# The order of the delta rule's pairs of heads: 1, 2, 0, 3 in place of 1, 2, 3, 0

## The chip, the cores and the metric

The kernel runs on one core of a Trainium2 chip. The metric is the time of one execution on the device in microseconds (us), smaller is better. A core has TensorE (PE; its weight loads are listed apart as PEld), VectorE (DVE), ScalarE (ACT), GpSimd (POOL) and SyncE (SP), which here issues nearly all DMAs; 16 DMA engines carry them out. TensorE's clock has two levels, 1.2 and 2.4 GHz; the profile gives the granted share of the full one.

## What is computed

One layer of a decoder for 288 tokens (256 of a prompt, and 8 sequences of 4 tokens with stored state) at width 2048, all in float32. A normed input is multiplied by one wide matrix `w_in`; the columns feed three mixers, whose outputs are gated, merged and followed by a feed-forward part:

```python
h = rmsnorm(x)                        # 288 x 2048
P = h @ w_in                          # 2048 x 16416: columns split among the mixers
# RetNet: rq 512, rk 512, rv 1024, rg 1024        (columns 0 to 3071)
# gated delta rule: q 1024, k 1024, v 1024         (3072 to 6143), da 8, db 8, dz 1024 (6160)
# GLA: lq 512, lk 512, lv 1024, llr 16, lg 1024    (7184 to 10271), then gates 6144
y_ret, y_gdn, y_gla = ...             # each 288 x 1024
merge = sum_i sigmoid(gate_i) * (branch_i @ w_branch[i])
x = x + merge @ w_o
x = x + SwiGLU(rmsnorm(x))
```

The gated delta rule has 8 heads of 128 columns. For each head q, k and v go through a convolution of width 4 over time and a SiLU, q and k are normed, and a state of 128 x 128 per sequence is read, used and written back. The heads don't depend on each other.

## The kernel before

Weights stream from HBM once. A product `x_in` (256 columns of `w_in`) is made by `products`: it loads four pieces `raw` of 512 KB (each 128 partitions x 4 rows x 256 columns, so 1 KB at a time out of rows of 16,416 x 4 = 65,664 bytes), splits each into a high and a low float32r part (`wh` by a ScalarE cast, L422; `wl` by a VectorE subtraction, L135), and multiplies with three matmuls per block (L129), 96 matmuls of 128 x 128 x 288 in all. `halves` does the same for 512 columns, in pieces of 2 KB. Four `raw` buffers are there, so the loads run at most four pieces ahead; SyncE issues them, in the order of its queue, with the state loads and stores and the small transfers between them.

`run` goes through four rounds. Each calls `self.gdn(ORDER[n])` for a pair of heads and then half of RetNet or GLA: (RetNet 1), (RetNet 0), (GLA 1), (GLA 0). `gdn(pair)` makes four products, for q, k, v (`gdn_conv`, columns 3072, 4096 and 5120 plus 256 x pair) and the gate (`gated`, columns 6160 plus 256 x pair), and then starts a generator `gdn_mix` with the delta rule itself. RetNet and GLA make a query and a key product and two of 512 columns, and start generators for their heads too. The generators do their small steps between the dense matmuls: `pump` advances them once per block of the following products. So the delta rule of one pair runs beside the products that follow it, and beside the delta products of the third round run RetNet's last heads, beside those of the fourth GLA's first heads.

`ORDER[0]` stays the same and is used three times more: the first pair's query weights are loaded in `setup`, and `gates` follows its second product. A pair number enters only as a column, row or index: in the weight columns, in the state (`state_gdn[0, :, h]`, 512 KB a head, loaded and stored by SyncE), in the convolution's state rows (ScalarE's queue, 24 KB), and in the block `ys[1, h]` of a scratch tensor in HBM to which `finish` writes a head's output. `branch(1, ...)` reads these blocks in the order of heads 0 to 7, after `branch(0, ...)`; the first two of these reads are issued early, as two `yr` buffers come free. For GLA, `gla` loads sums of the forget gate from HBM (`ev<-fsum`, L1279), and every head's state goes through four buffers `s0`, so that a state load (L659, L1073) waits for an earlier state's store to land.

The order of instructions on each engine is made by a scheduler from dependencies and modelled lengths; the program is one straight line without branches.

Of the kernel before, what the change touches and what calls it, by code (L numbers as in the profile page):

```python
# [39 lines left out]
R1 = 4  # L40
R2 = 6
EV = 9
ORDER = (1, 2, 3, 0)

O_RQ, O_RK, O_RV, O_RG = 0, 512, 1024, 2048
O_GQ, O_GK, O_GV = 3072, 4096, 5120
# [51 lines left out]
def blocks(t):  # L98
    return [t[:, k] for k in range(t.shape[1])]


class Trunk:
# [74 lines left out]
    def setup(self):  # L177
# [24 lines left out]
        for n in range(D // XC):  # L202
# [7 lines left out]
            ks = slice(2 * (n % 2), 2 * (n % 2) + 2)  # L210
            nc.sync.dma_start(out=raw[:, ks], in_=self.w_in(O_GQ + ORDER[0] * CHUNK)[:, 2 * n:2 * n + 2])
        xd = self.t(self.dr, (KT, P, T), "xT")
# [42 lines left out]
        for _ in range(2):  # L255
            next(steps)
        self.early = self.products(blocks(self.xh), blocks(self.xl), self.w_in(O_GQ + ORDER[0] * CHUNK), KT, False, steps, False)
        ra = self.t(x0, (112, P), "ra")
# [699 lines left out]
    def gdn(self, pair):  # L958
        q = self.gdn_conv(pair, 0)
        k = self.gdn_conv(pair, 1)  # L960
        if pair == ORDER[0]:
            self.gates()
# [486 lines left out]
    def run(self):  # L1449
# [7 lines left out]
        for n, (f, pair) in enumerate(((self.ret, 1), (self.ret, 0), (self.gla, 1), (self.gla, 0))):  # L1457
            self.gdn(ORDER[n])
            if n == 0:
# [67 lines left out]
```

## Time and profile before

| | us |
|---|---|
| median of 3 runs | 2231.0 (2226.45 to 2235.02) |
| profiled execution | 2233.02 |
| its span | 2231.2 |
| second round: pair 2 and RetNet 0, from the first matmul of its first product | 204.8 to 385.1 |
| third round: pair 3 and GLA 1 | 385.1 to 569.5 |
| fourth round: pair 0 and GLA 0 | 569.5 to 767.0 |

A round's stages below begin with the first matmul of a product. The rows are from one profiled execution. A window row gives its length, then for each engine its busy time and the number of instructions, then the granted share of TensorE's clock (PEclk), the mean busy share of the 16 DMA engines, and the GB/s that they moved. In a waits row the first engine stood idle until the second was done: us in total, times, longest. In a timeline row the numbers are start and length, and in brackets the idle time before it and what ended it. Matmuls overlap, so one that is listed with 0.29 us starts 0.13 us after the one before.

### The profile page before, as it was taken

The page shows a single profiled execution, that of the slowest core. Times are in us where ns is not written, and L with a number is a line of the kernel's source. Part 1 is how long each engine was busy: PE and PEld are TensorE (multiplying, and loading weights), DVE is VectorE, ACT ScalarE, POOL GpSimd, SP SyncE. Part 2 cuts the span into 40 slices and gives each one's busy share as a digit, 9 for nine tenths or more (in the row PEclk, how much of TensorE's full clock was granted, in tenths as well). Part 3 has the DMA queues.
Part 4 walks back from the last instruction along what each step waited for, and adds up shares of the span by engine and source line. Part 5 has one row for each costly group of instructions (what it writes and reads, how often), then busy time and mean ns, then how long its engine had stood idle before and what let it go on. Part 6 is the DMA issues. An engine that isn't in the chain of part 4 may idle for free.

```text
span 2231.2 us, 43877 instructions
## 1 busy us (share of the span) xinstructions
PE 2173.9 (97%) x17020; PEld 2114.5 (95%) x17020; DVE 1350.2 (61%) x2952; ACT 1028.7 (46%) x2114; POOL 211.7 (9%) x264
## 2 busy tenths in 40 slices
PE   8999989999998999999999999999999999999997
PEld 7899989989888999999999999999999999999997
DVE  6876775685686586555565655565555445556544
ACT  5645543553454355444444444444444334444443
POOL 2102301231343042000000000000000000000000
PEclk9999999999999999999999999999999999999998
DMA  8737985865997666677676566555555555555553
GB/s 232 159 117 160 159 177 115 196 168 127 129 135 181 122 197 185 190 188 186 176 191 164 169 183 187 176 163 169 166 165 168 164 169 162 170 162 169 162 161 118
DMA packets 251512, 370.24 MB, mean 166 GB/s; under 512 B 20318, under 2 KB 120248, under 8 KB 251144
## 3 DMA queue, kind: packets, MB, share of 16 engines
q1 hardware_dynamic: 249200, 364.04, 64.0%
q8 instruction: 133, 2.18, 0.4%
q0 software_dynamic: 896, 2.45, 0.3%
q10 hardware_dynamic: 1208, 0.96, 0.2%
q14 instruction: 75, 0.61, 0.1%
HBM read 341.70 MB, written 25.69 MB: 165 GB/s over the span
## 4 chain that ended last, share of the span: by engine, by line
PE 87%; DMA 8%; DVE 2%; ACT 1%; issue 1%; SPq 1%; POOL 0%; POOLq 0%; DVEq 0%; ACTq 0%
PE pd L129 54%; PE pm L129 32%; DMA raw<-in_w_in_dram 5%; PE pm L126 1%; DMA yr<-ys 1%; DMA out_dram<-s 1%; DVE wl L135 1%; DMA ev<-fsum 1%; ACT wh L422 0%; DMA xb<-in_x_sample_dram 0%; DMA s<-in_state_ret_dram 0%; DVE r L135 0%; DVE r L144 0%; SPq L204 0%; POOL r L1220 0%
## 5 line engine op out<-in xcount | busy, mean ns | idle before, releaser
L135 DVE TENSOR_TENSOR wl<-raw,wh 128x512 fp32r<-128x512 f32 (+1 forms) x1208 | 839.8, 698 | 711.1 <-ACT wh L386 491.0
L129 PE MATMUL pd<-xh,wh 128*128 128x288 f32 x2768 | 825.8, 300 | 22.2 <-ACT wh L422 14.5
L129 PE MATMUL pd<-xl,wh 128*128 128x288 f32 x2768 | 825.5, 299 | 0.0
L129 PE MATMUL pd<-xh,wl 128*128 128x288 f32 x2768 | 817.3, 299 | 1.6 <-DVE wl L135 1.6
L386 ACT CAST wh<-raw 128x512 fp32r<-128x512 f32 x784 | 485.1, 620 | 645.8 <-PE pd L129 332.9
L129 PEld LDWEIGHTS pd<-xh,wh 128*128 128x128 f32 x2768 | 524.5, 190 | 28.1 <-ACT wh L422 15.3
L129 PEld LDWEIGHTS pd<-xl,wh 128*128 128x128 f32 x2768 | 525.5, 190 | 3.5 <-issue 1.2
L129 PEld LDWEIGHTS pd<-xh,wl 128*128 128x128 f32 x2768 | 521.3, 190 | 6.4 <-DVE wl L135 3.5
L355 ACT CAST wh<-raw 128x512 fp32r<-128x512 f32 x224 | 137.8, 618 | 202.3 <-PE pd L129 187.0
L129 PE MATMUL pm<-xh,wl 128*128 128x288 f32 x704 | 207.8, 295 | 0.0
L129 PE MATMUL pm<-xl,wh 128*128 128x288 f32 x704 | 207.3, 294 | 0.0
L129 PE MATMUL pm<-xh,wh 128*128 128x288 f32 x704 | 207.0, 294 | 0.0
L422 ACT CAST wh<-raw 128x512 fp32r<-128x512 f32 x192 | 117.8, 621 | 93.7 <-PE pd L129 53.9
L129 PEld LDWEIGHTS pm<-xh,wl 128*128 128x128 f32 x704 | 132.1, 188 | 0.0
L129 PEld LDWEIGHTS pm<-xh,wh 128*128 128x128 f32 x704 | 132.1, 188 | 0.0
L129 PEld LDWEIGHTS pm<-xl,wh 128*128 128x128 f32 x704 | 132.0, 188 | 0.0
L129 PE MATMUL pd<-ah,wl 128*128 128x288 f32 x352 | 103.9, 295 | 0.0
L129 PE MATMUL pm<-ah,wl 128*128 128x288 f32 x352 | 103.9, 295 | 0.0
L129 PE MATMUL pm<-al,wh 128*128 128x288 f32 x352 | 103.8, 295 | 0.0
L129 PE MATMUL pd<-al,wh 128*128 128x288 f32 x352 | 103.7, 295 | 0.0
L129 PE MATMUL pm<-ah,wh 128*128 128x288 f32 x352 | 103.7, 295 | 0.0
L129 PE MATMUL pd<-ah,wh 128*128 128x288 f32 x352 | 103.6, 294 | 0.0
(372 smaller groups left out, 2921.1 us busy)
## 6 DMA issues: line engine op xcount, KB each, us to landing
raw<-in_w_in_dram SPq DMA_DIRECT2D x252, 512.0 KB
raw<-in_w_gate_up_dram SPq DMA_DIRECT2D x176, 512.0 KB
raw<-in_w_down_dram SPq DMA_DIRECT2D x88, 512.0 KB
raw<-in_w_branch_dram SPq DMA_DIRECT2D x48, 512.0 KB
raw<-in_w_o_dram SPq DMA_DIRECT2D x32, 512.0 KB
out_dram<-s SPq DMA_DIRECT2D x16, 512.0 KB
s<-in_state_gdn_dram SPq DMA_DIRECT2D x8, 512.0 KB
s<-in_state_ret_dram SPq DMA_DIRECT2D x16, 256.0 KB
```

What stands on the lines that cost most here:

```text
L126: self.nc.tensor.transpose(out, in_, self.ident[:k, :k])
L129: self.nc.tensor.matmul(out, lhsT=lhsT, rhs=rhs, start=start, stop=stop)
L135: self.nc.vector.tensor_tensor(out, a, b, op=op)
L355: nc.scalar.copy(wh, src)
L386: nc.scalar.copy(wh, raw[:, k])
L422: nc.scalar.copy(h, src)
```

## The change

The delta rule's pairs run in the order 1, 2, 0, 3. The third round takes pair 0 and the fourth pair 3; the first two rounds, RetNet and GLA stay. The last pair to be written to `ys` is then that of heads 6 and 7.

```diff
@@ -40,7 +40,7 @@
 R1 = 4
 R2 = 6
 EV = 9
-ORDER = (1, 2, 3, 0)
+ORDER = (1, 2, 0, 3)
 
 O_RQ, O_RK, O_RV, O_RG = 0, 512, 1024, 2048
 O_GQ, O_GK, O_GV = 3072, 4096, 5120
```

## Rows read from the trace of the kernel before

**Rows 1.** Page, part 1: busy us (share of the span) xinstructions of each engine.

```profile
PE 2173.9 (97%) x17020; PEld 2114.5 (95%) x17020; DVE 1350.2 (61%) x2952; ACT 1028.7 (46%) x2114; POOL 211.7 (9%) x264
```

**Rows 2.** Page, part 4: the chain that ended last, by line.

```profile
PE pd L129 54%; PE pm L129 32%; DMA raw<-in_w_in_dram 5%; PE pm L126 1%; DMA yr<-ys 1%; DMA out_dram<-s 1%; DVE wl L135 1%; DMA ev<-fsum 1%; ACT wh L422 0%; DMA xb<-in_x_sample_dram 0%; DMA s<-in_state_ret_dram 0%; DVE r L135 0%; DVE r L144 0%; SPq L204 0%; POOL r L1220 0%
```

**Rows 3.** Windows by stage, rounds three and four: us, busy (x) by engine, PEclk, DMA, GB/s.

```profile
385.10:455.40 70.30, 70.30 (x509) 66.53 (x508) 51.32 (x133) 37.09 (x91) 22.57 (x25) 1.00 0.84 191
455.40:499.70 44.30, 38.75 (x271) 34.94 (x270) 36.89 (x124) 25.56 (x77) 16.01 (x19) 0.92 0.64 166
569.50:655.00 85.50, 79.80 (x578) 73.67 (x577) 62.24 (x181) 38.29 (x95) 27.09 (x38) 0.98 1.00 133
655.00:702.50 47.50, 37.99 (x262) 34.51 (x261) 33.01 (x88) 24.39 (x75) 16.57 (x15) 0.93 0.77 177
```

**Rows 4.** Waits in pair 3's stage, 385.1 to 455.4: us in total, times, longest us.

```profile
ACT wh L422 <- DMA raw<-in_w_in_dram: 0.8, 1, 0.8
```

**Rows 5.** Waits in pair 0's stage, 569.5 to 655.0.

```profile
ACT wh L422 <- DMA raw<-in_w_in_dram: 14.6, 8, 5.7
```

**Rows 6.** Windows with 1 KB weight loads: pair 3, pair 0, RetNet's query (column 0).

```profile
371.00:391.00 20.00, 20.00 (x148) 18.12 (x147) 14.09 (x39) 10.08 (x31) 7.44 (x7) 1.00 0.45 92
550.00:570.00 20.00, 20.00 (x150) 17.97 (x150) 12.04 (x33) 9.51 (x28) 6.21 (x7) 1.00 1.00 84
258.00:275.00 17.00, 17.00 (x123) 15.76 (x121) 13.12 (x37) 8.43 (x18) 3.91 (x4) 1.00 0.90 84
```

**Rows 7.** Timeline of SyncE's DMA issues, 531 to 564: start us, us, what, xcount.

```profile
531.20 10.36 SPq L347 DMA_DIRECT2D raw<-in_w_in_dram  x4
547.54 16.02 SPq L325 DMA_DIRECT2D raw<-in_w_in_dram  x4
```

**Rows 8.** Windows with 2 KB weight loads: RetNet's second round, GLA's third.

```profile
303.00:361.00 58.00, 57.56 (x647) 54.82 (x646) 39.92 (x106) 20.17 (x39) 0.57 (x2) 1.00 0.70 142
496.00:545.00 49.00, 49.00 (x604) 46.75 (x603) 30.47 (x82) 18.08 (x36) 5.68 (x8) 1.00 0.47 139
```

**Rows 9.** Windows from a pair's first load to its last: pair 3, pair 0.

```profile
363.00:434.00 71.00, 71.00 (x529) 66.89 (x528) 43.83 (x117) 35.80 (x90) 18.67 (x22) 1.00 0.72 159
547.50:643.90 96.40, 90.81 (x668) 83.36 (x669) 63.47 (x187) 44.51 (x116) 31.46 (x44) 0.98 0.98 123
```

**Rows 10.** Timeline of ScalarE: the cast of pair 0's last load.

```profile
643.98 0.62 ACT L422 CAST wh<-raw 128x512 fp32r<-128x512 f32 x1 [0.20 <-DMA raw<-in_w_in_dram]
```

**Rows 11.** Timeline of TensorE: small matmuls of GLA's heads in pair 0's stage.

```profile
596.57 1.05 PE L129 MATMUL pm<-r 128*128 128x128 f32 x8
600.78 0.33 PE L129 MATMUL pm<-r 128*32 128x32 f32 x8 [2.63 <-DVE st L1249]
```

**Rows 12.** Timeline of the fourth round: the forget sums and who waits.

```profile
671.38 1.11 SPq L1279 DMA_DIRECT2D ev<-fsum  x1
679.35 0.23 ACT L132 ACTIVATE geb<-ev 128x32 f32<-128x32 f32 x1 [12.33 <-DMA ev<-fsum]
680.14 0.61 PE L129 MATMUL pd<-xh,wh 128*128 128x288 f32 x1 [8.03 <-ACT wh L422]
```

**Rows 13.** Window behind that stand: PEclk is the granted clock.

```profile
677.00:683.80 6.80, 3.66 (x14) 3.44 (x15) 3.54 (x9) 4.02 (x11) 0.07 (x1) 0.50 0.49 113
```

**Rows 14.** Timeline of the third round: the same load and its waiters.

```profile
480.68 0.50 SPq L1279 DMA_DIRECT2D ev<-fsum  x1
486.55 0.35 ACT L132 ACTIVATE geb<-ev 128x32 f32<-128x32 f32 x2 [1.35 <-DMA ev<-fsum]
488.75 0.55 PE L126 MATMUL pm<-ident,ev 128*128 128x128 f32 x3 [1.73 <-DVE ev L144]
```

**Rows 15.** Timeline of SyncE: the branches' blocks written (L649) and read (L1297).

```profile
804.80 0.92 SPq L649 DMA_DIRECT2D ys<-yo  x2
822.11 3.83 SPq L1297 DMA_DIRECT2D yr<-ys  x2
```

## The prediction

> **What bounds the kernel now.** I read the page first: TensorE is busy 97% of the span and matmuls are 86% of the chain that ended last, but 5% of that chain is weight loads out of `w_in`, the largest other item [rows 1, 2]. So the mean says "TensorE" and one stage may say something else. The rounds of `run` (one pair of the delta rule, then half of RetNet or GLA) all issue the same dense products, so I cut the span at the first matmul of each product and compared rounds [rows 3]. The reader is to see that the third round's delta stage (pair 3) takes 70.3 us at a DMA share of 0.84, and the fourth round's (pair 0) 85.5 us at a share of 1.00 and *fewer* GB/s (133 against 191). The waits agree: ScalarE's weight casts wait 0.8 us for loads in pair 3's stage and 14.6 us in pair 0's [rows 4, 5].
>
> Why are pair 0's loads slow? Two stretches hold weight loads alone [rows 6]: for pair 3 the DMA engines move 92 GB/s at a share of 0.45, so 92/0.45 = 204 GB/s while they work; for pair 0 it is 84 GB/s at a share of 1.00. Nothing else is issued by SyncE between 531 and 564 us [rows 7], so it isn't company that slows them. What differs is the address: each load takes 1 KB pieces of rows of 16,416 columns, pair p starting at column 256p of its block; pair 0 starts at 3072, 4096, 5120 (multiples of 1024) and 6160 (16 past one), pair 3 768 further. RetNet's query product of the second round starts at column 0, another multiple of 1024, and moves 84 GB/s at 0.90, so 93 [rows 6]. Pieces of 2 KB show it too: starts 1024 and 2048 move 142/0.70 = 203 GB/s, starts 8720 and 9760 (528 and 544 past a multiple) 139/0.47 = 296 [rows 8]. So I take the slowness as the address's, and expect it to go where pair 0 goes.
>
> The Trainium skill, "DMA: Bandwidth & Descriptors", section "Latency and other measured facts", says that copies slow down where partitions lie a large power of two apart in HBM, and that padding by 192 B didn't cure it. This pitch is 64 KiB + 128 B, so by that rule alone all four pairs, which share the pitch, would be equally slow and the order worth 0 (2231). Here the trace disagrees: at one pitch it shows 204 and 84 GB/s, and by these rows I go.
>
> **The change part by part.** No instruction is added or removed; in the third and fourth rounds pair 0 and pair 3 change places. What moves with a pair is its 16 weight loads of 512 KB, two loads and two stores of state, the convolution's small state rows, and the addresses of its outputs.
>
> (a) *Pair 0 in the third round.* From its first load to its last, pair 3's loads and what goes with them take 0.72 x 71.0 = 51.1 us of all 16 engines; pair 0's take 0.98 x 96.4 = 94.5 [rows 9]; the end at 643.9 is the last one's cast, which waited for it [rows 10]. The lead is the same in both rounds: first load to first matmul is 385.1 - 363.0 = 22.1 and 569.5 - 547.5 = 22.0 us [rows 3, 9]. So the supply would again end 96.4 us after 363.0, at 459.4; TensorE needs the 655.0 - 643.9 = 11.1 us after it that it needs now, and the stage ends at 470.5 in place of 455.4: +15.1. The low bound comes from TensorE's work: pair 0's stage holds 578 - 509 = 69 more matmuls than pair 3's [rows 3], since GLA's heads run beside it, and at 0.04 to 0.13 us each (0.33/8 and 1.05/8, [rows 11]) 3 to 9 us of its extra 15.2 are that work, not the loads; the loads alone would then be worth 15.2 - 9 = +6. I take +14, near the supply's figure, because the share stood at 0.98 to 1.00 throughout. Bounds +6 and +16.
>
> (b) *Pair 3 in the fourth round.* Its loads and what goes with them want 51 us of the DMA engines in a stage of over 70, so they no longer bind, and the work does: 70.3 us plus those 3 to 9, so 73 to 79 in place of 85.5: -12 to -6. Middle: -9.5.
>
> (c) *The two products behind each stage.* Query and key of GLA take 44.3 us in the third round and 47.5 in the fourth [rows 3]. In the fourth round the query loads (column 7184, 16 past a multiple) stay slow, but they start with a full lead instead of a spent one; up to the difference of 3.2 can come back. I take -1.5. In the third round the fast query loads now follow a spent lead: 0 to +3.2, I take +1. Behind this lies a wait that neither bound holds: ScalarE must read GLA's forget sums (`ev<-fsum`), which SyncE issues behind stores of state, and weight casts stand behind it in ScalarE's queue. In the fourth round that load is issued at 671.4, ScalarE goes on at 679.4 and TensorE stands 8.0 us [rows 12], after which its clock is granted at 0.50 for 6.8 us (the 1.2 GHz level after an idle stretch, 3.4 us of work lost) [rows 13]. In the third round the load comes back within 5.9 us and costs TensorE 1.7 [rows 14]. It is priced with the rivals.
>
> (d) *Edits at nothing.* The blocks that the second branch reads first (heads 0 and 1) are written by the last pair now, at 804.8, and read at 822.1 [rows 15]: 17 us of cover. After the change heads 6 and 7 are last written, and the reads that want them are the last two of that branch's eight, so no cover shrinks. State loads and stores keep their size and their place; no row shows one to be slow by its head, so 0, with 1 us either way. SyncE issues the same queue in the same order as long as the scheduler, which orders by dependencies and lengths, sees no difference; I see none before the reads at 822.1.
>
> Sum: +14 - 9.5 - 1.5 + 1 = +4. Low: 6 - 12 - 3.2 + 0 - 1 = -10. High: 16 - 6 + 0 + 3.2 + 1 = +14. The profiled execution took 2233.0 us (span 2231.2 and 1.8 around it), 2.0 over the median of 2231.0. So 2233.0 + 4 - 2 = 2235 beside that median, bounds 2221 and 2245.
>
> **The rivals.**
> *Place, not address.* The fourth round is slow because of what runs there, and the order is worth 0: 2231. For it: the 69 extra matmuls are the place's. Against it: loads alone at 84 GB/s [rows 6, 7]. Chance 0.12. (The Trainium skill's rule of the pitch, above, would end here too.)
>
> *Faster.* The five slow products in a row (pair 0's four and GLA's query) are cut into four and one. With its lead back, the fourth round's query stage runs ahead, the forget sums come back as fast as in the third round, and the stand of 8.0 with its 3.4 of slow clock goes: -11.4 in place of -1.5, so 4 - 9.9 = -6: 2225; with (a) at its low bound, 2217. For it: in the third round the same load costs 1.7. Against it: the query's own loads stay slow and share the queue with it. Chance 0.16.
>
> *Slower.* The third round takes over the stand: behind a full queue the forget sums need 8 us and not 5.9, TensorE idles 8.0 instead of 1.7 and its clock falls for 6.8 us, +6.3 + 3.4, while the fourth keeps its own and (b) yields only 6: 15.1 + 9.7 - 6 + 1 = +20: 2251; half of it, 2241. It decides at a DMA share near 1 when that load is issued. For it: state stores and loads already hold SyncE there. Against it: with fast query loads before it the queue should have emptied. Chance 0.17.
>
> *Not what it says.* The scheduler places SyncE's queue otherwise: within 10 us of either side. Chance 0.05.
>
> **How the numbers follow.** The forecast has 0.50: 2235. About 0.5%, 11 us, is what a measurement of this kernel can tell from no change: faster is under 2220, slower over 2242. The forecast gives 0.03 to faster and 0.07 to slower, the faster rival 0.07 of its 0.16, the slower one 0.11 of its 0.17, the scheduler 0.01 each way: 0.11 faster, 0.19 slower, 0.70 within. Range: the sum's bounds, 2221 to 2245, with 1 us more below for the faster rival's tail and 2 more above, towards the middle of the slower rival (2241 to 2251): 2220 to 2247.
>
> **What would show it.** (a): in the third round a DMA share near 1 at 120 to 135 GB/s, a stage of 82 to 87 us and casts waiting some 15 us for loads. (b): the fourth round's stage at 73 to 79 us with under 3 us of such waits. (c): where `ev<-fsum` lands and how long TensorE stands behind it, in both rounds. Wrong would be: pair 0's loads at 200 GB/s in the third round (place), or a third round as long as before with a shorter fourth (then the slow loads hide there), or different orders of instructions beyond the swap.

## The result, and the profile after

The changed kernel is slower: 2248.6 us median against 2235.2 for the kernel before on the same chips, a ratio of 1.0060 (95% interval 1.0046 to 1.0074), so 13.4 us. The forecast was 2235 beside 2231 (+4) and its range ended at 2247, 16 us over that median. The kernel before ran 4 us slower in this comparison than in the three runs of the forecast, so the change itself is what to compare: +13.4 against +4. The sign and the mechanism held, one term was too small. The profiled execution of after has a span of 2250.4 us.

Its windows, cut as in [rows 3] at the first matmul of each product; between them the loads' own windows, cut as in [rows 9]. The columns are those of [rows 3]: us, busy us of PE, PEld, DVE, ACT and POOL with (x instructions), PEclk, DMA share, GB/s.

```profile
370.00:472.60 102.60, 89.28 (x604) 81.75 (x602) 49.68 (x134) 37.55 (x96) 22.76 (x24) 0.93 0.99 118
392.10:485.10 93.00, 79.51 (x510) 73.03 (x508) 50.33 (x131) 35.56 (x90) 24.27 (x24) 0.91 1.01 147
485.10:530.20 45.10, 40.23 (x270) 36.49 (x270) 38.63 (x126) 25.82 (x79) 16.91 (x19) 0.89 0.65 169
600.00:676.70 76.70, 76.70 (x578) 72.09 (x577) 65.45 (x185) 41.39 (x102) 27.10 (x39) 1.00 0.74 141
676.70:722.40 45.70, 37.91 (x263) 34.78 (x262) 32.49 (x85) 22.31 (x69) 15.73 (x15) 0.93 0.81 183
578.00:658.00 80.00, 80.00 (x611) 74.61 (x611) 59.81 (x169) 40.47 (x104) 29.45 (x41) 1.00 0.62 140
```

The first row runs from pair 0's first load to the landing of its last, the last row the same for pair 3. The table sets the stages against those of [rows 3]; GLA's value and gate products, which follow, took 69.8 us in the third round of both kernels.

| stage | before | after | difference | forecast |
|---|---|---|---|---|
| third round, delta | 70.3 (pair 3) | 93.0 (pair 0) | +22.7 | +14 (+6 to +16) |
| third round, GLA's query and key | 44.3 | 45.1 | +0.8 | +1 (0 to +3.2) |
| fourth round, delta | 85.5 (pair 0) | 76.7 (pair 3) | -8.8 | -9.5 (-12 to -6) |
| fourth round, GLA's query and key | 47.5 | 45.7 | -1.8 | -1.5 (-3.2 to 0) |
| sum | | | +12.9 | +4 |

The sum, +12.9, is close to the difference of the medians, 13.4. The two profiles also differ by 6 us before the second round (204.8 and 210.8 us to its first matmul), where both programs are the same; in the profiles of this study that stretch took 201 to 213 us whatever the kernel did later. So I compare stages, not spans: with the same columns and company the third round's delta stage repeats within 0.2 us from profile to profile. The others repeat less well. Query and key in `a_w3` below take 46.3 us in the third round, where the kernel before took 44.3 behind the same fast columns, and 46.8 in the fourth, where after took 45.7; so +0.8 and -1.8 in the table are hardly more than the spread. The fourth round's delta stage with slow columns spreads too, from 84.6 us (`c_3210` below, which leaves that round as it was) over 85.5 here to 86.7 (`b_w0`).

What the third round's stage waits for, and the forget sums in both rounds (the waits of after, 392.1 to 485.1; then the timelines of ScalarE and TensorE, one line of the third round and two of the fourth):

```profile
ACT wh L422 <- DMA raw<-in_w_in_dram: 42.4, 11, 7.1
DVE wl L135 <- ACT wh L422: 40.0, 13, 7.6
```

```profile
516.55 0.35 ACT L132 ACTIVATE geb<-ev 128x32 f32<-128x32 f32 x2 [1.04 <-DMA ev<-fsum]
...
698.99 0.23 ACT L132 ACTIVATE geb<-ev 128x32 f32<-128x32 f32 x1 [11.26 <-DMA ev<-fsum]
699.78 0.61 PE L129 MATMUL pd<-xh,wh 128*128 128x288 f32 x1 [7.54 <-ACT wh L422]
```

ScalarE's casts wait 42.4 us for weight loads in pair 0's stage, where [rows 4] has 0.8 for pair 3 and [rows 5] 14.6 for pair 0 in the fourth round. The stand behind the forget sums (8.0 us in [rows 12]) is still there in the fourth round, 7.5 us, and in the third ScalarE waits 1.04 us for them, in place of 1.35 [rows 14]: nothing was taken over and hardly anything given back.

### The profile page after: what moved, and what is told of

It reads as the page before. It is cut to its first block, busy times and chain, and to the rows that moved or that the text cites. A ratio compares the mean times of both kernels' runs of the same rounds, so it can differ in the third digit from the quotient of the medians.

```text
span 2250.4 us, 43877 instructions
## 1 busy us (share of the span) xinstructions
PE 2184.0 (97%) x17020; PEld 2123.5 (94%) x17020; DVE 1353.0 (60%) x2952; ACT 1030.9 (46%) x2114; POOL 214.0 (10%) x264
## 4 chain that ended last, share of the span: by engine, by line
PE 85%; DMA 8%; DVE 4%; ACT 1%; issue 1%; POOL 0%; SPq 0%; ACTq 0%; POOLq 0%; DVEq 0%
PE pd L129 52%; PE pm L129 31%; DMA raw<-in_w_in_dram 6%; DVE wl L135 1%; PE pm L126 1%; DMA yr<-ys 1%; DVE r L144 1%; ACT wh L422 0%; DMA ev<-fsum 0%; DVE ev L144 0%; DMA rm<-in_norm_mix_dram 0%; DVE s L144 0%; DVE ev L135 0%; DMA yr<-accd 0%; DMA cmask<-in_c_lv_dram 0%
```

## Experiments: does the price go with the weights' columns?

Three kernels let a pair read another pair's weight columns and move nothing else. This is the edit of `b_w3` (kernel before); `a_w3` (kernel after) has the same with its own `ORDER`, `b_w0` (kernel before) has `{3: 0}`. Here and below a diff shows the lines that matter, without their surroundings:

```diff
-ORDER = (1, 2, 3, 0)
+ORDER = (1, 2, 3, 0); WCOL = {0: 3}
-        self.x_in(O_GQ + c0, ev)
+        self.x_in(O_GQ + part * 1024 + WCOL.get(pair, pair) * CHUNK, ev)
-        sz = self.gated(2, O_DZ + pair * CHUNK)
+        sz = self.gated(2, O_DZ + WCOL.get(pair, pair) * CHUNK)
```

> The kernel before, in which pair 0 (fourth round) multiplies with pair 3's columns of w_in for query, key, value and gate, so that pair 0 of the output is computed from the wrong weights; nothing else changes. Address theory (the cost sits in the start columns of the weight loads): the fourth round's delta stage falls from 85.5 us to about 76.7, the query and key products behind it from 47.5 to about 45.6, as in the changed kernel's fourth round: 11 us less, ratio 0.995 to the kernel before. Place theory (the fourth round is slow because GLA's heads run beside it): 85.5 stays, ratio 1.000.

> The kernel after, in which pair 0 (now in the third round) multiplies with pair 3's columns of w_in, so that pair 0 of the output is computed from the wrong weights; the states, the outputs' addresses and the order stay those of the kernel after. Its weight addresses are then those of the run before it, column for column. Address theory: the third round's delta stage falls from 93.0 us to about 70.3 and the whole equals the run before it, ratio 0.995 to the kernel before. If something else that moves with a pair costs (its states, the convolution's rows, the outputs' blocks): the third stage stays above 73 and the ratio between 0.997 and 1.006.

> The kernel before, in which pair 3 (third round) multiplies with pair 0's columns of w_in, so that pair 3 of the output is computed from the wrong weights; both rounds then read slow columns and no head moves. Address theory: the third round's delta stage rises from 70.3 us to what the changed kernel shows there, 93.0, query and key behind it by 0.8, and the fourth keeps its 85.5: 23.5 us more, ratio 1.0105. If the 8 us beyond the +14 of the prediction come from something else that the swap moves: +14 to +15, ratio 1.0065. Place theory: 1.000.

Measured, to the kernel before: `b_w3` 0.9931 (0.9913 to 0.9948), `a_w3` 0.9945 (0.9926 to 0.9963), `b_w0` 1.0095 (1.0080 to 1.0111). The windows of the third and the fourth round's delta stage, first of `b_w3`:

```profile
383.90:454.20 70.30, 70.30 (x509) 66.53 (x508) 50.97 (x133) 37.19 (x91) 23.03 (x25) 1.00 0.82 190
569.60:646.30 76.70, 76.70 (x578) 72.09 (x577) 65.42 (x185) 41.32 (x102) 27.00 (x39) 1.00 0.75 141
```

of `a_w3`, with its query and key stages as the last two lines:

```profile
384.30:454.60 70.30, 70.30 (x509) 66.53 (x508) 51.17 (x133) 37.18 (x91) 23.03 (x25) 1.00 0.83 190
570.70:647.40 76.70, 76.70 (x578) 72.09 (x577) 65.44 (x185) 41.38 (x102) 27.07 (x39) 1.00 0.74 141
454.60:500.90 46.30, 40.21 (x271) 36.40 (x270) 37.72 (x125) 25.89 (x77) 15.81 (x19) 0.89 0.64 161
647.40:694.20 46.80, 38.63 (x263) 35.47 (x262) 32.13 (x85) 22.30 (x69) 15.91 (x15) 0.89 0.80 180
```

and of `b_w0`, with the loads' window of the third round between:

```profile
382.10:475.10 93.00, 77.06 (x509) 70.61 (x507) 50.21 (x131) 35.27 (x90) 23.27 (x24) 0.94 1.00 148
360.00:462.40 102.40, 88.37 (x605) 80.95 (x605) 49.89 (x134) 37.49 (x96) 22.79 (x24) 0.95 0.99 119
590.30:677.00 86.70, 81.45 (x579) 76.05 (x578) 61.62 (x182) 39.32 (x97) 27.17 (x38) 0.94 1.00 135
```

(`b_w3` gained 15 us by its medians and 9 by its stages, 8.8 and 0.5. The spread of the start is large enough for the rest, but no profile shows that it is the rest.) The reader is to see four numbers that come back in these kernels and in those before and after: with fast columns the third round's stage takes 70.3 us and the fourth's 76.7, with TensorE busy throughout (PE busy equals the window); with slow columns 93.0 and 85.5 to 86.7, at a DMA share of 1. `a_w3` has the swapped order and `b_w3` the old one, and with the same columns these stages are equal. So heads, states, convolution rows and the blocks of `ys` cost nothing that these stages show where they moved (step d), and the whole change is the start columns of 16 loads, seen in a round where they cost 22.7 in place of one where they cost 9.

That also says why the round matters: a stage ends with the later of its work and its loads. The work is 70.3 us in the third round and 76.7 in the fourth; the slow loads end near the same time after they begin, so the round with less work shows more of them. But "near the same time" was wrong by 6 us: 102.6 us from the first load to the last landing in the third round (102.4 in `b_w0`), 96.4 in the fourth [rows 9].

## Experiments: why the slow loads end 6 us later in the third round

The company differs. In the third round's stage SyncE loads the state of RetNet's head 1 (1 MB), in the fourth's that of GLA's head 3 (1 MB). RetNet's goes in four transfers over 64 partitions each, every second row; GLA's in two over 128. `a_flat` takes the gap between the state's pieces away, `a_two` gives RetNet's state GLA's shape, `a_nost` leaves the load out, and `a_part` leaves out three quarters of its bytes. All edit the kernel after:

```diff
 a_flat
-            hv = hbm.rearrange("b (k two) e -> two k b e", two=2)
+            hv = hbm.rearrange("b (two k) e -> two k b e" if h == 1 else "b (k two) e -> two k b e", two=2)
 a_two: s_in
-            return perm(t, self.i["state_ret"][0, bs, h])
+            return [(t, self.i["state_ret"][0, bs, h].rearrange("b k e -> k b e"))] if h == 1 else perm(t, self.i["state_ret"][0, bs, h])
 a_nost: s_in, then wide_state
-            return perm(t, self.i["state_ret"][0, bs, h])
+            return [(t, None)] if h == 1 else perm(t, self.i["state_ret"][0, bs, h])
-                self.nc.sync.dma_start(out=dst, in_=src)
+            for dst, src in state_in(s, slice(4 * z, 4 * z + 4)): self.nc.sync.dma_start(out=dst, in_=src) if src is not None else self.nc.gpsimd.memset(dst, 0.0)
 a_part: s_in, then wide_state (part is h == 1)
-            return perm(t, self.i["state_ret"][0, bs, h])
+            return [(d[:, 0:1], x[:, 0:1]) if h == 1 else (d, x) for d, x in perm(t, self.i["state_ret"][0, bs, h])]
+            self.nc.gpsimd.memset(s[:, 1:], 0.0) if part else None
```

> The kernel after, in which the state of RetNet's head 1, which is read and written in the third round's delta stage, is addressed by halves of its rows (1 KB pieces 1 KB apart) instead of by every second row (1 KB pieces 2 KB apart): the same eight transfers of 256 KB and the same pieces, and head 1's state rows are exchanged among each other. Theory S (the delta stage is dearer in the third round than the prediction's 85 us because RetNet's state pieces, 2 KB apart, are slow company for the slow weight loads): the third stage falls from 93.0 us to 85 to 88, ratio to the kernel before 1.002 to 1.004. Rival (any company costs the same there, or the stage is long because of TensorE's own idle stretches and clock falls): 92 to 94 us, ratio 1.006.

> The kernel after without the load of the state of RetNet's head 1 (1 MB in four transfers, in the third round's delta stage); GpSimd sets that tile to zero instead, so head 1's state output is computed from zero. Every engine's order of work stays. Theory C (the third round's slow loads end 102.6 us after their start and not 96.4 as in the fourth round of before, because RetNet's state in their company costs more DMA time than GLA's there): without the 1 MB the loads end at most 96 us after their start and the third stage falls from 93.0 to 86 us or less. Rival (the slow weight loads alone set the pace, 16 loads at 6.2 us each make 99 us, and company is carried beside them at nothing): 91 to 93 us still.

> The kernel after, in which the state of RetNet's head 1 is loaded in the shape that GLA's has: two transfers of 512 KB over 128 partitions in place of four of 256 KB over 64, so head 1 starts from state rows in another order. The bytes, the 1 KB pieces and every engine's order stay. Theory C1 (RetNet's state is dearer company than GLA's because of its four transfers over 64 partitions): the third round's delta stage falls from 93.0 us to 86 to 88 and the loads end about 96 us after their start. Rival C2 (1 MB of state costs some 6 us beside slow loads in any shape): 92 to 94 us.

> The kernel after, in which each of the four transfers that load the state of RetNet's head 1 brings one batch of four (64 KB in place of 256 KB, 0.25 MB in all) and GpSimd sets the rest to zero, so head 1 starts from a part of its state. SyncE keeps its queue: it still stands until the state's buffer is free, with weight loads behind it. Theory B (the bytes beside slow weights cost): a quarter of the 6.3 us stays, the third round's delta stage is 87.5 to 89 us. Theory H (SyncE's stand in its queue costs, whatever it then brings): 92 to 93.5 us.

Measured, the third round's stage and under it the loads' window. `a_flat` (ratio to the kernel before 1.0049, 1.0032 to 1.0067):

```profile
384.90:478.10 93.20, 78.35 (x510) 71.92 (x508) 50.11 (x131) 35.65 (x90) 24.02 (x24) 0.93 1.01 148
362.80:465.40 102.60, 88.00 (x594) 80.78 (x593) 49.26 (x134) 37.54 (x97) 22.44 (x24) 0.93 1.00 119
```

`a_nost` (1.0036, 1.0016 to 1.0055):

```profile
392.90:479.60 86.70, 76.51 (x509) 70.42 (x508) 49.49 (x132) 35.71 (x91) 25.43 (x27) 0.94 0.98 144
370.80:466.90 96.10, 85.91 (x602) 78.58 (x601) 48.67 (x132) 37.47 (x96) 23.57 (x26) 0.96 0.98 117
```

`a_two` and `a_part` (one run each):

```profile
382.50:473.40 90.90, 77.15 (x509) 70.86 (x507) 50.07 (x131) 35.48 (x90) 24.18 (x24) 0.92 1.00 152
360.40:460.70 100.30, 86.70 (x592) 79.63 (x591) 49.23 (x132) 37.37 (x96) 22.76 (x24) 0.93 0.98 121
```

```profile
385.50:474.20 88.70, 76.88 (x509) 70.46 (x507) 49.90 (x131) 35.19 (x90) 24.48 (x26) 0.94 0.98 144
363.40:461.50 98.10, 88.02 (x604) 80.64 (x604) 49.06 (x133) 37.44 (x96) 23.29 (x26) 0.95 0.98 117
```

The distance between the state's pieces falls as a cause: 93.2. The load itself stands: without the 1 MB the loads end 96.1 us after their start and the stage takes 86.7, a little over the 96 and 86 that theory C named, so this company costs 6.3 us of the stage; with a quarter of it 2.0 us are back (88.7). `a_part` also tells its bytes from SyncE's queue, whose timeline in after and in `a_part` reads (start us, us, what):

```profile
407.55 6.53 SPq L325 DMA_DIRECT2D raw<-in_w_in_dram  x1
415.58 3.21 SPq L1073 DMA_DIRECT2D s<-in_state_ret_dram  x3
418.89 2.15 SPq L325 DMA_DIRECT2D raw<-in_w_in_dram  x1
```

```profile
400.20 6.72 SPq L325 DMA_DIRECT2D raw<-in_w_in_dram  x1
408.42 1.97 SPq L1072 DMA_DIRECT2D s<-in_state_ret_dram  x3
410.49 0.53 SPq L325 DMA_DIRECT2D raw<-in_w_in_dram  x1
```

In both, SyncE issues a weight load, stands for the state's buffer, issues three of the state's transfers, and only then the next weight load, 11.3 us after the one before it in after and 10.3 in `a_part`. The stand is 1.0 us shorter, yet the stage is 4.3 us shorter, where theory B put it (87.5 to 89) and not at 92 to 93.5; the 2.0 us that are left belong to a quarter of the bytes and to the stand together. GLA's shape gives 2.1 us of the 6.3; between the two theories for `a_two` (86 to 88, and 92 to 94) neither number came.

Two kernels put the same question to the fourth round of the kernel before: `b_nogla` leaves out the load of GLA's state there, `b_four` gives it RetNet's shape.

```diff
 b_nogla: gla_head; wide_state as in a_nost
-        s0 = self.wide_state(lambda t, bs_: [(t, io(self.i["state_gla"], bs_))])
+        s0 = self.wide_state(lambda t, bs_: [(t, None if h == 3 else io(self.i["state_gla"], bs_))])
 b_four: gla_head
-        s0 = self.wide_state(lambda t, bs_: [(t, io(self.i["state_gla"], bs_))])
+        s0 = self.wide_state(lambda t, bs_: [(t[64 * u:64 * u + 64], self.i["state_gla"][0, bs_, h].rearrange("b (k two) e -> two k b e", two=2)[u]) for u in range(2)] if h == 3 else [(t, io(self.i["state_gla"], bs_))])
```

> The kernel before without the load of the state of GLA's head 3 (1 MB in two transfers, in the fourth round's delta stage); GpSimd sets the tile to zero, so that head is computed from a zero state. Theory C1 (GLA's state is cheap company, RetNet's dear): the fourth stage stays at 84.5 to 86 us. Rival C2 (1 MB costs some 6 us in either round): it falls to 78 to 80 us.

> The kernel before, in which the state of GLA's head 3 (fourth round's delta stage) is loaded in the shape that RetNet's has: four transfers of 256 KB over 64 partitions, every second row, in place of two of 512 KB over 128; that head starts from its state rows in another order. The bytes and the work stay. If the shape has a price of its own (2.1 us in the third round): the fourth stage goes from 85.5 to about 87.6 us. If not, and the third round's 2.1 came from where the transfers fell: 85 to 86 us.

`b_nogla`, one run: the fourth round's stage, the loads' window, a row of the stage's waits, and the timelines of GpSimd, ScalarE and TensorE in it:

```profile
567.20:652.60 85.40, 79.52 (x578) 74.17 (x577) 65.76 (x185) 40.86 (x102) 28.32 (x41) 0.96 1.02 120
545.20:638.70 93.50, 87.62 (x645) 80.85 (x646) 64.30 (x185) 44.13 (x114) 31.25 (x44) 0.96 1.00 112
```

```profile
ACT wh L422 <- DMA raw<-in_w_in_dram: 7.0, 2, 4.3
```

```profile
593.08 0.95 POOL L1072 MEMSET s<- 128x1024 f32 x1 [5.92 <-DMA out_dram<-s]
...
594.79 0.42 ACT L132 ACTIVATE r<-r 128x256 f32<-128x256 f32 x1 [6.50 <-POOL r L1221]
...
596.03 1.37 PE L126 MATMUL pm<-ident,yk 128*128 128x128 f32 x4 [5.47 <-ACT yk L132]
```

By its stage (85.4) the run says that GLA's state is free, but the stage can't be read that way: the edit moved the wait for the state's buffer from SyncE to GpSimd, where GLA's own steps (L1220, L1221) stand behind it, ScalarE waited 6.5 us for these, and TensorE 5.5 us for ScalarE. The loads end 93.5 us after their start in place of 96.4. That is a price for GLA's 1 MB only from below, 2.9 us or more, against 6.5 (102.6 - 96.1) for RetNet's: the casts waited for loads only twice in this stage, where they did so eight times before [rows 5], so the later loads were held up by casts that freed their buffers late, and might have ended earlier. `b_four`, one run:

```profile
577.70:662.00 84.30, 79.74 (x577) 74.28 (x577) 62.23 (x181) 38.80 (x95) 27.18 (x38) 0.96 1.00 135
555.70:651.20 95.50, 91.01 (x669) 84.24 (x669) 63.79 (x186) 45.00 (x116) 31.86 (x44) 0.96 0.99 124
```

RetNet's shape costs nothing that shows in the fourth round (84.3 against 85.5, 95.5 against 96.4; the stage spreads by 2 us without it). So the shape alone doesn't make the difference, and the 2.1 us of `a_two` may come from where its transfers fell. What is shown: in the third round 1 MB of RetNet's state costs the slow loads 6.5 us, and even without it they end hardly sooner than the fourth round's do with GLA's (96.1 against 96.4). How the 6.2 us between the rounds divide is not shown, since the price of GLA's 1 MB is known only from below and from a single run: if it costs 2.9 us, RetNet's is 3.6 dearer and other transfers make 2.6; if it costs as much as RetNet's, the other transfers make all of it. Decay (128 KB) and RetNet's stores are candidates by the list of transfers; no run left them out.

## Experiments: where the slow columns lie, and two ways to load them otherwise

```diff
 b_map (kernel before)
-ORDER = (1, 2, 3, 0)
+ORDER = (1, 2, 3, 0); SHIFT = {3: (64, 128, 192, 384), 0: (512, 640, 896, 960)}
-        self.x_in(O_GQ + c0, ev)
+        self.x_in(O_GQ + (part * 1024 + SHIFT[pair][part] if pair in SHIFT else c0), ev)
-        sz = self.gated(2, O_DZ + pair * CHUNK)
+        sz = self.gated(2, O_DZ - 16 + SHIFT[pair][3] if pair in SHIFT else O_DZ + pair * CHUNK)
```

> The kernel before, in which the query, key, value and gate weights of pair 3 (third round) are read from columns 64, 128, 192 and 384 past a multiple of 1024, and those of pair 0 (fourth round) from 512, 640, 896 and 960 past one, so that both pairs are computed from wrong weights. It maps the slowness over the start column. If it falls off with the distance from a multiple of 1024: a load of 512 KB takes about 6 us of all engines near 0 and 960, 2.6 us at 512 to 768, between them a slope; then the third stage stands between 70.3 and 93.0 us and the fourth near 77. If only exact multiples (0 to 32) are slow: 70.3 and 76.7.

One run: the third round's stage took 73.1 us and the fourth's 76.7 (the first two rows). The other rows are windows in which hardly anything but weight loads ran, for starts of 64, 128, 512 and 960 past a multiple of 1024:

```profile
381.40:454.50 73.10, 70.51 (x510) 66.54 (x509) 50.58 (x133) 36.92 (x91) 22.95 (x25) 1.00 0.79 185
567.90:644.60 76.70, 76.70 (x578) 72.11 (x577) 65.48 (x185) 41.34 (x102) 27.15 (x39) 1.00 0.92 140
361.00:379.60 18.60, 18.60 (x146) 16.76 (x145) 9.06 (x22) 8.10 (x24) 2.88 (x4) 1.00 0.69 94
381.50:390.00 8.50, 8.50 (x61) 7.99 (x60) 8.50 (x27) 4.26 (x10) 5.25 (x5) 1.00 0.57 137
547.00:566.00 19.00, 19.00 (x146) 17.13 (x144) 10.36 (x28) 9.03 (x26) 3.84 (x5) 1.00 0.59 110
602.00:617.00 15.00, 15.00 (x113) 14.22 (x112) 13.38 (x39) 8.94 (x23) 6.89 (x9) 1.00 0.87 81
```

GB/s over share, as in the prediction: 136 at 64, 240 at 128, 186 at 512, 93 at 960, beside 84 at 0 and 204 at 768 [rows 6]. So the slow columns lie on both sides of a multiple of 1024: slow at 64 before it (960), less slow at 64 after it, and fast at 128 after it. It is neither a slope over the whole range nor the exact multiple alone; how far the strip reaches before the multiple is not shown. (192, 384, 640 and 896 ran among state loads and stores and have no clean window.)

`b_half` and `b_quart` issue each slow load of the kernel before in two halves of its partitions or in four blocks of rows (each loop stands on one line there):

```diff
-            self.nc.sync.dma_start(out=raw[:, :kn], in_=src)
+            for ps in ((slice(0, 64), slice(64, P)) if split else (slice(0, P),)):        # b_half
+                self.nc.sync.dma_start(out=raw[ps, :kn], in_=src[ps])
+            for ks in ([slice(z, z + 1) for z in range(kn)] if split else [slice(0, kn)]):  # b_quart
+                self.nc.sync.dma_start(out=raw[:, ks], in_=src[:, ks])
```

> The kernel before, in which every 512 KB weight load of 1 KB pieces that starts on a slow column (0, 16 or 32 past a multiple of 1024) is issued as two transfers of 64 partitions each; the output is the same. If the slowness comes from which rows the 16 DMA engines read at the same moment (they then stand 4 rows apart instead of 8), the fourth round's stage changes clearly: towards 77 us (ratio down to 0.995) or, where the new spacing is worse, over 90 us. If it sits in each 1 KB piece whatever stands beside it: 85.5 us plus at most 1 us for the doubled issues, ratio 1.000.

> The kernel before, in which each of those slow loads is issued as four transfers of 128 KB, one for each block of 128 rows; the output is the same. In a single transfer an engine's pieces of one partition lie 128 rows apart; split, consecutive pieces lie one row apart. If the order of the pieces on an engine makes them slow: the fourth stage goes towards 77 us, ratio 0.995. If not: 85.5 us plus up to 2 us for the issues, ratio 1.000.

`b_half` gave 1.0047 (1.0029 to 1.0066) and `b_quart` 1.0047 (1.0028 to 1.0065). Their fourth stages:

```profile
571.20:657.50 86.30, 79.39 (x568) 74.43 (x567) 59.75 (x175) 38.92 (x96) 26.27 (x38) 0.94 1.02 130
572.40:663.20 90.80, 78.02 (x568) 72.71 (x567) 59.48 (x173) 38.55 (x96) 25.15 (x38) 0.96 1.02 124
```

Neither makes the loads faster: the share stays at 1 and the GB/s, 130 and 124, don't pass the 133 of [rows 3]. Both are slower by more than was expected. The scheduler also moved some small work in both (568 matmuls in the stage in place of 578), so the loss isn't the issues' alone. How the 16 engines share out a transfer's rows shows in no run, so the spacings that the first expectation names are assumed.

## Experiments: orders that avoid the price

If a stage is the later of work and loads, slow products belong where they have a full lead and work beside them. Three orders tried on the kernel before; the first two edits are of the tuple that `run` goes through:

```diff
 b_gla01
-(self.ret, 1), (self.ret, 0), (self.gla, 1), (self.gla, 0)
+(self.ret, 1), (self.ret, 0), (self.gla, 0), (self.gla, 1)
 c_both
+(self.ret, 0), (self.ret, 1), (self.gla, 0), (self.gla, 1)
 c_3210
-ORDER = (1, 2, 3, 0)
+ORDER = (3, 2, 1, 0)
```

> The kernel before with GLA's pairs of heads in the order 0, 1 in place of 1, 0; the output is the same. The slow query loads (column 7184) then come in the third round behind pair 3's fast loads, and the fourth round's query (column 7440, 272 past a multiple) follows pair 0's slow ones. Supply theory (a stage is as long as the later of its work and its loads): the third round's query and key keep their 44 us plus 0 to 3, the fourth's 47.5 fall to 44 to 46, the rest stays: 0 to 3 us less, ratio 0.999 to 1.000. If GLA's slow queries cost more where the rounds stand otherwise: 1.002 or more.

> The kernel before with the delta rule's pairs in the order 3, 2, 1, 0; the output is the same. Pair 0 stays in the fourth round, where slow loads cost least, and pair 1 (256 past a multiple, between slow and fast) goes from the first round, where its casts wait 11 us for loads, to the third. Supply theory: the first round gains up to 8 us with pair 3's fast loads, the third loses 0 to 3 (starts of 64 to 384 made it 73.1 in place of 70.3), the fourth stays at 85.5: ratio 0.997 to 1.001. If the first round's waits are those of the start and not of the addresses: 1.000 to 1.002.

> The kernel before with GLA's pairs and RetNet's pairs both in the order 0, 1 in place of 1, 0; the output is the same. With GLA's alone the ratio was 0.997: its slow query loads cost 5 us more in the third round and 10 us less in the fourth. RetNet's slow query (column 0) moves from the second round to the first. Supply theory: the second round's query and key fall from 42.3 us towards 37, the first round's rise from 31.8 to 32 to 37, so -5 to +1 on top: ratio 0.994 to 0.998. If the first round, whose loads start from nothing, has no slack for slow ones: 0.998 to 1.002.

`c_3210`: 1.0005 (0.9995 to 1.0014), no difference. Its third round has pair 1, whose columns start 256 past a multiple, and takes the 70.3 us of a fast pair; its fourth has pair 0:

```profile
381.70:452.00 70.30, 70.30 (x509) 66.53 (x509) 51.17 (x133) 37.09 (x91) 22.59 (x25) 1.00 0.80 191
566.10:650.70 84.60, 80.37 (x578) 74.84 (x577) 62.80 (x181) 38.60 (x95) 27.19 (x38) 0.96 1.00 134
```

So pair 1's loads are not between slow and fast, as the expectation had it. `b_gla01`: 0.9972 (0.9961 to 0.9983). `c_both`: 0.9934 (0.9913 to 0.9956), 2219.8 us beside 2233.5, the fastest of the three orders and a little under the 0.994 expected; its second round's query and key take 34.6 us in place of 42.3. GLA's query and key in `b_gla01`, third and fourth round, then the second round's query and key in `c_both` and the fourth round's:

```profile
453.90:503.40 49.50, 41.98 (x272) 36.85 (x271) 36.58 (x122) 25.68 (x78) 16.07 (x19) 0.86 0.81 180
658.40:695.60 37.20, 35.83 (x263) 32.97 (x262) 33.70 (x88) 22.36 (x70) 16.14 (x15) 1.00 0.75 211
275.10:309.70 34.60, 33.40 (x249) 31.02 (x248) 27.91 (x98) 20.17 (x61) 5.24 (x4) 1.00 0.70 192
654.40:691.50 37.10, 35.75 (x262) 32.88 (x261) 33.59 (x88) 22.31 (x69) 16.08 (x15) 1.00 0.73 210
```

The third round's rise from 44.3 us to 49.5, more than the 3 expected, and the fourth's fall from 47.5 to 37.2, far more than the 1.5 to 3.5. What makes the third round's surplus was not followed up. The surplus in the fourth round is the stand behind the forget sums. In `b_gla01` their load is issued 7 us after the stage's first matmul in place of 16 [rows 12], it has nearly come back when ScalarE needs it, the 12.3 us of [rows 12] are 1.5, and the granted clock stays at 1.00:

```profile
665.48 0.65 SPq L1279 DMA_DIRECT2D ev<-fsum  x1
...
671.67 0.23 ACT L132 ACTIVATE geb<-ev 128x32 f32<-128x32 f32 x1 [1.51 <-DMA ev<-fsum]
```

So the gain that the prediction's faster rival named (-11.4 in that stage) exists (-10.3 here); it came when GLA's pair with the slow query left the fourth round, and pair 0's loads could stay. The states and the other columns of that pair moved with the query; no run moved the query's columns alone.

## Why the prediction was wrong, point by point

**The step that failed is (a)**, pair 0's price in the third round: +14 taken, bounds +6 and +16, +22.7 measured. Its parts: 1.1 us were given away by taking 14 in place of the supply figure 15.1; the loads ended 102.6 us after their start in place of 96.4 (+6.2); TensorE needed 12.5 us after the last landing (485.1 - 472.6) in place of 11.1 (+1.4). That is 8.7, the whole miss of (a). The 6.2 came from carrying "the loads and what goes with them" from one round to another as one block of DMA time. What goes with them is not the pair's: it is the transfers of whichever head runs beside. In the third round the load of RetNet's state alone cost the slow loads 6.5 us (`a_nost`); how much of the 6.2 is that it is dearer than GLA's (at most 3.6) and how much is other transfers (at least 2.6) stays open.

**The low bound of (a)** was wrong in kind. It subtracted the fourth round's extra work, 3 to 9 us, from the price of the loads. By `b_w3` that work is 6.4 us (76.7 - 70.3), but it lies beside the waiting and covers it: the fourth round showed 8.8 us of the slow loads *because* it had more work, and the third shows more for having less. The bounds that the rows allowed were others: a stage of 85.4 us from the end of the loads as the low one, with the work of 70.3 well under it, and above it a high one with room for unlike company.

**(b) and (d) held**: -8.8 against -9.5, and nothing else moved (the delta stages of `a_w3` equal those of `b_w3`). **(c)** came out at -1.8 and +0.8 against -1.5 and +1, but terms so small are not told from the spread of these stages, so it is neither borne out nor refuted. That the slowness goes with the start column held too: the share stood at 1 in the third round (118 GB/s over the loads and 147 over the stage, on either side of the 120 to 135 named), and pair 3 took the fourth round in 76.7 with no wait for loads among the longer ones. The stage of 82 to 87 us and the 15 us of waits were missed (93.0 and 42.4).

**The rivals.** Place alone is out: `b_w3` gained with every head in its old place. By the rule of the pitch from the Trainium skill ("DMA: Bandwidth & Descriptors", "Latency and other measured facts") the pairs would have been alike, though the page's own figures are for pitches of 512 KiB and more and this one is far under them; no run agrees, since at one pitch the start column alone moved a stage by 22.7 us. The slower rival reached the measured time (2241 to 2251) by another way: it had the third round take over the forget sums' stand, which didn't happen (ScalarE's wait for them was 1.04 us there). The faster rival fell, and its own counter-argument, that the query's slow loads share the queue with the sums, fits `b_gla01`, where the sums are issued sooner once that pair of GLA's is gone.

## What to carry over

Price a moved transfer at its new place: take the later of the work there and the loads there, and build the loads' time from what is queued beside them in that round, not from the round they came from. Where two rounds differ in work, the one with more work hides more of a slow load, so the surplus work of the old place is no discount on the new one. Slow loads in a row can also be broken up by reordering something else that is free to move: here the order of GLA's and RetNet's pairs gave 0.7%, about what this swap cost.

## What the runs showed of the hardware

1 KB pieces out of rows of 65,664 bytes are slow by their start column alone: per busy share of the DMA engines they moved 84 GB/s at a multiple of 1024 columns (4 KB), 136 at 64 past one, 240 at 128, 186 at 512, 204 at 768 and 93 at 960 (one run for 64, 128, 512 and 960). Moving the columns and nothing else changed a stage from 70.3 to 93.0 us (`b_w0`). Issuing them in smaller transfers, by partitions or by blocks of rows, doesn't help (86.3 and 90.8 us against 85.5). Fast transfers in their company are not carried for nothing: the load of 1 MB of state ended the slow loads 6.5 us later in the third round (`a_nost`), at a DMA share near 1 with it and without.
